# Down projections of a two-layer decoder trunk: 10 of 22 row blocks as 2x2 block products with seven multiplications, placed among the gate and up products of later chunks

## The chip, the cores and the metric

The kernel runs on 1 core of one Trainium2 chip. The metric is the device time of one execution in microseconds, as the median of several runs; one further execution was taken with the hardware profiler, and its trace is what this text reads.

## The reference

The trunk has two layers over 256 tokens of width 1024. Each layer is a feed-forward block (FFN), a mixer and a second FFN, each followed by a layer norm. The change is in the four FFNs, each of which is `swiglu` with 2816 hidden columns.

```python
def swiglu(x, w_gu, w_down):
    g, u = jnp.split(x @ w_gu, 2, axis=-1)
    return (jax.nn.silu(g) * u) @ w_down

def reference(x, ln_g, ln_b, ffn_w_gu, ffn_w_down, ...):
    for l in range(DEPTH):                       # 2
        x = layer_norm(ALPHA * x + 0.5 * swiglu(x, ffn_w_gu[l, 0], ffn_w_down[l, 0]), ln_g[l, 0], ln_b[l, 0])
        ...                                      # y: attention and gating (layer 0), mLSTM (layer 1)
        x = layer_norm(ALPHA * x + y, ln_g[l, 1], ln_b[l, 1])
        x = layer_norm(ALPHA * x + 0.5 * swiglu(x, ffn_w_gu[l, 1], ffn_w_down[l, 1]), ln_g[l, 2], ln_b[l, 2])
    return x
```

## The kernel before

All activations stay on the chip: `xTh` and `xTl` hold the transposed activation (1024 x 256), `xn` the natural one (2 halves `t` of 128 tokens x 1024). Every large product is made of three matmuls (`mm3`): each fp32 operand is split in a high part rounded to fp32r and a low part that is the rest, and high x high, high x low and low x high are summed in PSUM. The weights' split is work on the chip too: `split` lets ACT cast the high part (`whi`) and DVE subtract it (`wlo`).

**Weights** come as a stream `W` of blocks of 128 x 1024 (512 KB), numbered `n` in the order in which TensorE (PE) uses them. `w_dma(n)` loads a block into one of `RAW` = 6 buffers on SP's queue, `w_split(n)` splits it into one of `RING` = 9 slots (`whi`, `wlo`), and `w_done(n)`, called when the last matmul of a block has been written down, splits block n + 9 and loads block n + 15. So a slot that PE frees is refilled at once with the block that PE wants nine blocks later.

**An FFN** (`ffn`) has 22 chunks of 128 hidden columns. The first 2 or 4 are made as groups (`post`), while the previous layer norm ends. `chunk(c)` makes one of the others: 24 matmuls of 256 columns for gate into a PSUM bank of tag `m` (3 banks), a silu on ACT, 24 for up, the product of the two on DVE (tile `hp`), and its split into the `hT` of that chunk. Then `out_proj` is the down projection: for each of the 22 row blocks c and each half t of the tokens, `hT[c, t]` is the stationary operand and 512 columns of the weight block the moving one, 12 matmuls of 512 columns for a block, into four PSUM banks of tag `a` (`acc[t][h]`). The last 7 blocks (`skew`) are taken bank by bank, so that the layer norm of one half starts while PE still works on the other.

**The other parts** are `layer_norm` (DVE, with its transposes on PE into tag `a`), `mixer_ab` and `mixer_c`; side work is written as generators that `tick` advances between products. The instructions of PE, DVE, ACT and GpSimd are put in their final order by the framework's scheduler from priorities in the order of the code; the order on SP is that of the code. `page` gives one of `PAGES` = 26 buffers of 516 columns.

Of the kernel before, what the change touches and what calls it, by code (L numbers as in the profile page):

```python
# [14 lines left out]
P = 128  # L15
# [5 lines left out]
FC = 22  # L21
ALPHA = 4.0 ** 0.25
EPS = 1e-5
RING = 9
RAW = 6
PAGES = 26
NWARM = 7


@with_exitstack  # L30
def trunk(ctx, tc, W, F_d, x_d, g_d, b_d, rope_d, id_d, idb_d, mk_d, tri_d, sel_d,
# [125 lines left out]
    def feed(i):  # L157
        if i < KC:
            st[i] = wpool.tile([P, 1024], F32, tag="raw", name="raw", bufs=RAW)
            if i == 0:  # L160
                nc.sync.dma_start(out=st[i][:, 0:256], in_=F_d[i][:, 0:256])
                nc.scalar.dma_start(out=st[i][:, 256:768], in_=F_d[i][:, 256:768])
            else:
                nc.sync.dma_start(out=st[i][:, 0:768], in_=F_d[i])
        else:
            w_dma(i - KC + 4)

    for i in range(RAW):
        feed(i)
# [1 line left out]
    for i in range(KC):  # L171
        j, o = divmod(i, 2)
        if o == 0:
            whi[j] = wpool.tile([P, 1024], F32R, tag="hi", name="whi", bufs=RING)
            wlo[j] = wpool.tile([P, 1024], F32R, tag="lo", name="wlo", bufs=RING)
# [33 lines left out]
    def layer_norm(t, acc, scale, eps, k, last=False, segs=((0, 512), (512, 512))):  # L209
        st = small("lnst", [P, 3, 6])  # L210
        mv = small("lnmv", [P, 2])
        for i, (o, w) in enumerate(segs):
            if i < 2:
                sl = xn[:, t, i * 512:(i + 1) * 512]
                nc.vector.scalar_tensor_tensor(out=sl, in0=sl, scalar=scale, in1=acc[i], op0=OP.mult, op1=OP.add)  # L215
# [97 lines left out]
        return spawn(layer_norm(1, acc[1], scale, eps, k, last))  # L313

    def ffn(n0, k, ln_prev, last=False):
        hT = {}
        head = 1 if ln_prev is None else 2

        def post(g, t, ps):
            hp = pages.tile([P, 2, 256], F32, tag="h", name="hp", bufs=3)  # L320
# [9 lines left out]
            split(pt, q[:, 0], q[:, 1])  # L330

        def chunk(c):
            n = n0 + 4 * head + 2 * (c - 2 * head)
# [6 lines left out]
            nc.vector.tensor_tensor(out=hp[:, 1, :], in0=hp[:, 0, :], in1=pu, op=OP.mult)  # L340
            q = page("hT", [P, 2, S], F32R)
            split(hp[:, 1, :], q[:, 0], q[:, 1])
            for t in range(2):
                w = slice(t * P, (t + 1) * P)
                hT[c, t] = (q[:, 0, w], q[:, 1, w])
# [37 lines left out]
    def mixer_ab(n0, k, ln_prev):
        sgb = cpool.tile([P, 2, 512], F32, name="sgb")
# [4 lines left out]
        bcast(sgb[:, 0, :], sg_d, 0, 512)  # L389
        bcast(sgb[:, 1, :], sb_d, 0, 512)  # L390
# [95 lines left out]
        def sgu_v(ps, t):  # L486
# [71 lines left out]
    def mixer_c(n0, k, ln_prev):  # L558
        va, qkT, gate, num, cat, cc = {}, {}, {}, {}, {}, {}
        pTs, hst, done = {}, {}, set()  # L560
        hgp = cpool.tile([P, 2, 512], F32, name="sgb")
        hg = [hgp[:, i, :] for i in range(2)]
# [13 lines left out]
        def gates(ps):  # L576
# [16 lines left out]
            yield 2  # L593
# [172 lines left out]
def _arrays(np, i):  # L766
# [4 lines left out]

    def ffn(l, f, head):
        w = i["ffn_w_gu"][l, f]
        gu = w.reshape(4, 2, P, 2, FG, 256).transpose(4, 0, 2, 1, 3, 5)
        parts.append(gu[0:head].reshape(4 * head, P, 1024))
        gc = w.reshape(8, P, 2, FC, P).transpose(3, 2, 1, 0, 4)
        parts.append(gc[2 * head:].reshape(2 * (FC - 2 * head), P, 1024))
        parts.append(i["ffn_w_down"][l, f].reshape(FC, P, 1024))
# [83 lines left out]
```

## Time and profile before

| | |
|---|---|
| median of 3 runs | 969.52 us (969.33 to 969.57) |
| the profiled execution | 969.82 us, span of the instructions 968.1 us |
| PE busy | 956.7 us, 99% of the span |
| weight loads of PE (PEld) | 857.3 us, 89% |
| DVE busy | 599.1 us, 62% |
| ACT busy | 455.8 us, 47% |
| from HBM | 180.97 MB, 188 GB/s over the span |

The span is what the trace shows, from the first instruction of the program to the last; the execution's own time is 1.7 us longer. PE is called busy while a matmul is in flight, and one matmul's time in flight is longer than the step from its start to the next one's start, so a matmul's cost is read from starts.

### The profile page before, as it was taken

To read this page: it belongs to the slowest core of one execution; us is meant where nothing else is said; L and a number is where in the kernel's file an instruction comes from. 1 tells how busy PE (TensorE), PEld (TensorE's weight loads), DVE (VectorE), ACT (ScalarE), POOL (GpSimd) and SP (SyncE) were. 2 spreads that over 40 slices of the span, in tenths; PEclk is the share of its full clock that TensorE was granted. 3 is DMA by queue.
4 is the path that set the end of the run, shared out by engine and by line. 5 is a ranking of instruction groups with operands and counts; after the bars stand their busy time and mean duration, and the time that the engine had idled before them with its cause. 6 is when DMAs were issued, how large, how long until landed. Compare 5 with 4: busy or idle time off the path is not lost.

```text
span 968.1 us, 15564 instructions
## 1 busy us (share of the span) xinstructions
PE 956.7 (99%) x6226; PEld 857.3 (89%) x6226; DVE 599.1 (62%) x829; ACT 455.8 (47%) x657; POOL 22.3 (2%) x28
## 2 busy tenths in 40 slices
PE   9999999999999999999999999999999999999997
PEld 7999988887888999988889999888888789999885
DVE  7575554685777555544875555438767876555435
ACT  6564443345645444443354444325675445445320
POOL 0000000000100000000000000001000000000000
PEclk9999999999999999999999999999999999999999
DMA  9885666484446656666466565656644467666611
GB/s 349 307 299 182 192 188 187 159 275 150 140 135 219 225 190 183 194 186 188 169 238 181 191 191 182 194 152 219 217 131 126 137 216 230 187 194 182 189 45 44
DMA packets 52072, 183.03 MB, mean 189 GB/s; under 512 B 6176, under 2 KB 6688, under 8 KB 51872
## 3 DMA queue, kind: packets, MB, share of 16 engines
q1 hardware_dynamic: 51856, 181.77, 58.2%
q8 instruction: 49, 0.80, 0.3%
q10 hardware_dynamic: 144, 0.26, 0.1%
q14 instruction: 23, 0.19, 0.1%
HBM read 180.97 MB, written 1.05 MB: 188 GB/s over the span
## 4 chain that ended last, share of the span: by engine, by line
PE 70%; DVE 2%; POOL 0%; issue 0%; ACT 0%; DVEq 0%
PE ps_m L120 15%; PE ps_m L121 15%; PE ps_m L122 15%; PE ps_a L121 8%; PE ps_a L120 8%; PE ps_a L122 8%; DVE wlo L93 1%; PE ps_a L237 1%; POOL hrs L206 0%; PE ps_t L326 0%; ACT whi L92 0%; PE ps_a L503 0%; DVE hst L684 0%; DVE num L711 0%; PE ps_a L665 0%
## 5 line engine op out<-in xcount | busy, mean ns | idle before, releaser
L93 DVE TENSOR_TENSOR wlo<-raw,whi 128x1024 fp32r<-128x1024 f32 (+1 forms) x327 | 393.9, 1212 | 231.8 <-ACT whi L92 230.4
L92 ACT CAST whi<-raw 128x1024 fp32r<-128x1024 f32 (+1 forms) x327 | 339.9, 1043 | 378.4 <-PE ps_m L121 190.6
L120 PE MATMUL ps_m<-xTh,whi 128*128 128x256 f32 x1280 | 358.6, 280 | 1.4 <-DVE qkc L651 1.4
L121 PE MATMUL ps_m<-xTl,whi 128*128 128x256 f32 x1280 | 357.8, 280 | 0.0
L122 PE MATMUL ps_m<-xTh,wlo 128*128 128x256 f32 x1280 | 357.4, 279 | 0.0
L120 PEld LDWEIGHTS ps_m<-xTh,whi 128*128 128x128 f32 x1280 | 240.6, 188 | 2.1 <-ACT cch L92 1.6
L121 PEld LDWEIGHTS ps_m<-xTl,whi 128*128 128x128 f32 x1280 | 240.6, 188 | 0.6 <-issue 0.3
L122 PEld LDWEIGHTS ps_m<-xTh,wlo 128*128 128x128 f32 x1280 | 240.6, 188 | 0.2 <-issue 0.2
L120 PE MATMUL ps_a<-whi,hT 128*128 128x512 f32 (+1 forms) x352 | 138.2, 392 | 0.0
L121 PE MATMUL ps_a<-wlo,hT 128*128 128x512 f32 (+1 forms) x352 | 138.0, 392 | 0.0
L122 PE MATMUL ps_a<-whi,hT 128*128 128x512 f32 (+1 forms) x352 | 137.9, 392 | 0.0
L120 PE MATMUL ps_m<-whi,xTh 128*128 128x512 f32 x224 | 90.7, 405 | 0.0
L121 PE MATMUL ps_m<-wlo,xTh 128*128 128x512 f32 x224 | 89.3, 399 | 0.0
L122 PE MATMUL ps_m<-whi,xTl 128*128 128x512 f32 x224 | 88.6, 396 | 0.0
L122 PEld LDWEIGHTS ps_a<-whi,hT 128*128 128x128 f32 x352 | 66.1, 188 | 15.2
L120 PEld LDWEIGHTS ps_a<-whi,hT 128*128 128x128 f32 x352 | 66.1, 188 | 15.1
L121 PEld LDWEIGHTS ps_a<-wlo,hT 128*128 128x128 f32 x352 | 66.1, 188 | 15.0
L340 DVE TENSOR_TENSOR hp<-hp,ps_m 128x256 f32<-128x256 f32 x74 | 31.2, 421 | 51.0 <-PE ps_m L122 50.9
L122 PEld LDWEIGHTS ps_m<-whi,xTl 128*128 128x128 f32 x224 | 42.1, 188 | 9.6
L120 PEld LDWEIGHTS ps_m<-whi,xTh 128*128 128x128 f32 x224 | 42.2, 188 | 9.1
L121 PEld LDWEIGHTS ps_m<-wlo,xTh 128*128 128x128 f32 x224 | 42.2, 188 | 8.7
L215 DVE SCALAR_TENSOR_TENSOR xn<-xn,ps_a 128x512 f32<-128x512 f32 x24 | 16.0, 682 | 37.5 <-PE ps_a L122 37.4
(197 smaller groups left out, 601.3 us busy)
## 6 DMA issues: line engine op xcount, KB each, us to landing
raw<-in_W SPq DMA_DIRECT2D x320, 512.0 KB, 4.2
gb<-in_g SPq DMA_DIRECT2D x6, 512.0 KB, 3.9
gb<-in_b SPq DMA_DIRECT2D x6, 512.0 KB, 4.8
raw<-in_F SPq DMA_DIRECT2D x7, 384.0 KB, 5.5
xn<-in_x SPq DMA_DIRECT2D x1, 1024.0 KB
out<-xn SPq DMA_DIRECT2D x4, 256.0 KB, 2.0
swt<-in_sw SPq DMA_DIRECT2D x2, 256.0 KB, 7.7
sgb<-in_hg SPq DMA_DIRECT2D x2, 256.0 KB, 5.3
```

The costliest lines, as they stand in the source:

```text
L92: nc.scalar.copy(out=hi, in_=src)
L93: nc.vector.tensor_tensor(out=lo, in0=src, in1=hi.bitcast(F32), op=OP.subtract)
L120: mm_(out=out, lhsT=lh, rhs=rh, start=start, stop=False)
L121: mm_(out=out, lhsT=lh, rhs=rl, start=False, stop=False)
L122: mm_(out=out, lhsT=ll, rhs=rh, start=False, stop=stop)
L215: nc.vector.scalar_tensor_tensor(out=sl, in0=sl, scalar=scale, in1=acc[i], op0=OP.mult, op1=OP.add)
L237: nc.tensor.transpose(pt[:, c, :], sl[:, c * P:(c + 1) * P], ident)
L340: nc.vector.tensor_tensor(out=hp[:, 1, :], in0=hp[:, 0, :], in1=pu, op=OP.mult)
```

## The change

Blocks 4 to 13 of the 22 row blocks of each down projection leave `out_proj` and are taken in 5 pairs. Two row blocks (even chunk e, odd chunk o) times two halves of the tokens are a 2x2 block matrix of `hT`; two row blocks times two quarters of 256 output columns are a 2x2 block matrix of the weights. Their product, four 128 x 256 blocks, is made from seven block products in place of eight (the variant with 15 additions). Since the output has four quarters, a pair is taken twice, for `r` = 0 (columns 0 to 511) and `r` = 1 (512 to 1023): 20 pairs, 40 calls of `pair` in the kernel.

The additions on the hidden side are made in `chunk` (tile `hs`, four 128 x 128 operations after the odd chunk), those on the weights' side in `refill` (tile `tt`), and those on the results in `fold`, which adds the four banks of a round into `xn`. `ffn_plan` puts `pair(0, p)` behind chunk 7 + 2p and `pair(1, p)` behind chunk 16 + p. A paired weight block holds the four 128 x 256 quarters of both row blocks, and its split takes two slots: 768 columns of plain quarters and 1024 of sums. `RING` goes from 9 to 8, `RAW` from 6 to 5, `PAGES` from 26 to 30; `w_done` refills as many blocks as there are free slots. In `mixer_c` the generators `norm(t, 0)` are started behind the third chunk of the second group instead of behind the fourth of the first, and one `yield` is longer; the mixers' tiles `sgb` move into pages.

```diff
-RING = 9
-RAW = 6
-PAGES = 26
+RING = 8
+RAW = 5
+PAGES = 30
+NP = 5
+C0 = 4
...
+PAIRS = range(C0, C0 + 2 * NP, 2)
+PLAIN = [c for c in range(FC) if not C0 <= c < C0 + 2 * NP]
+SLOTS = {}
+for _p in range(NP):
+    SLOTS.setdefault(C0 + 2 * _p + 3, []).append((0, _p))
+    SLOTS.setdefault(C0 + 2 * NP + 2 + _p, []).append((1, _p))
...
+    def refill():
+        while ring["split"] < NG and ring["free"] >= (2 if paired(ring["split"]) else 1):
...
+            if paired(n):
+                yh, yl = slot()
+                tt = wpool.tile([P, 4, 256], F32, tag="tt", name="tt", bufs=TT)
+                bb = r.rearrange("p (a n) -> p a n", a=4)
+                sub = nc.vector.tensor_tensor
+                sub(out=tt[:, 0:2, :], in0=bb[:, 0:1, :].to_broadcast([P, 2, 256]), in1=bb[:, 1:3, :], op=OP.subtract)
+                split(r[:, 256:1024], hi[:, 0:768], lo[:, 0:768])
+                sub(out=tt[:, 2, :], in0=bb[:, 2, :], in1=tt[:, 0, :], op=OP.subtract)
+                sub(out=tt[:, 3, :], in0=bb[:, 3, :], in1=tt[:, 2, :], op=OP.subtract)
+                split(tt.rearrange("p a n -> p (a n)"), yh, yl)
...
     def w_done(n):
+        ring["free"] += 2 if paired(n) else 1
         del whi[n], wlo[n]
-        w_split(n + RING)
-        w_dma(n + RING + RAW)
+        refill()
...
+                tt(out=hs[:, 4, :], in0=hs[:, 0, :], in1=hs[:, 2, :], op=OP.add)
+                tt(out=hs[:, 5, :], in0=hs[:, 4, :], in1=hs[:, 1, :], op=OP.subtract)
+                tt(out=hs[:, 6, :], in0=hs[:, 0, :], in1=hs[:, 1, :], op=OP.subtract)
+                tt(out=hs[:, 7, :], in0=hs[:, 3, :], in1=hs[:, 5, :], op=OP.subtract)
+                for lo, hi in ((1, 5), (5, 8)):
...
+                    split(hs[:, lo:hi, :], qh, ql)
...
+        def pair(r, p):
+            n = at["pair", r, p]
+            if p == 0:
+                acc[r] = [bank_a((P, 2, 256)) for _ in range(4)]
+            a = acc[r]
+            for i, half, col, b, h in ((1, 0, 0, 2, 0), (3, 0, 2, 0, 0), (7, 0, 1, 0, 1), (2, 1, 3, 1, 0),
+                                       (4, 1, 0, 1, 1), (5, 1, 2, 2, 1), (6, 1, 1, 3, 0)):
+                w = slice(256 * col, 256 * col + 256)
+                rh, rl = whi[n][half][:, w], wlo[n][half][:, w]
+                lh, ll = hS[p, i]
+                o = a[b][:, h, :]
+                mm_(out=o, lhsT=lh, rhs=rh, start=p == 0 and h == 0, stop=False, skip_group_check=True)
+                mm_(out=o, lhsT=lh, rhs=rl, start=False, stop=False, skip_group_check=True)
+                mm_(out=o, lhsT=ll, rhs=rh, start=False, stop=p == NP - 1, skip_group_check=True)
+            w_done(n)
+            tick()
+            if p == NP - 1:
+                fold(r, a)
...
+            nc.scalar.copy(out=x[:, 0, :], in_=a[2][:, 0, :])
+            tt(out=u[:, 0, :], in0=x[:, 0, :], in1=a[2][:, 1, :], op=OP.add)
+            tt(out=u[:, 1, :], in0=u[:, 0, :], in1=a[3][:, 0, :], op=OP.add)
+            tt(out=x[:, 1, :], in0=u[:, 0, :], in1=a[1][:, 1, :], op=OP.add)
+            stt = nc.vector.scalar_tensor_tensor
+            stt(out=x0, in0=x0, scalar=2.0 * ALPHA, in1=a[1], op0=OP.mult, op1=OP.add)
+            stt(out=x1, in0=x1, scalar=2.0 * ALPHA, in1=a[0], op0=OP.mult, op1=OP.add)
+            tt(out=x0, in0=x0, in1=u[:, 1:2, :].to_broadcast([P, 2, 256]), op=OP.add)
+            tt(out=x1, in0=x1, in1=x, op=OP.add)
...
-        return out_proj(FC, n0 + 4 * FG, lhs, 7, k, 2.0 * ALPHA, 4.0 * EPS, last)
+        return out_proj(len(PLAIN), at["down", PLAIN[0]], lhs, 7, k, None, 4.0 * EPS, last)
...
-            for t in range(2):
-                norms[t, g] = spawn(norm(t, g))
...
+                if g == 1 and i == 2:
+                    for t in range(2):
+                        norms[t, 0] = spawn(norm(t, 0))
+            if g == 1:
+                for t in range(2):
+                    norms[t, 1] = spawn(norm(t, 1))
```

How the instructions stand is shown at three places. The first is PE in the second FFN, at the end of chunk 15 (bank `ps_m_4026` before, `ps_m_4435` now, its up product). Before, the gate product of chunk 16 follows at once:

```order
L122 MATMUL ps_m_4026<-xTh_72,wlo_3748 128x256
L120 MATMUL ps_m_4062<-xTh_72,whi_3779 128x256
L121 MATMUL ps_m_4062<-xTl_73,whi_3779 128x256
L122 MATMUL ps_m_4062<-xTh_72,wlo_3780 128x256
L120 MATMUL ps_m_4062<-xTh_72,whi_3779 128x256
```

Now the 21 matmuls of `pair(0, 4)` stand between the two; the first ten and the last one are:

```order
L171 MATMUL ps_m_4435<-xTh_72,wlo_4213 128x256
L429 MATMUL ps_a_3763<-whi_4272,hSh_4291 128x256
L430 MATMUL ps_a_3763<-wlo_4273,hSh_4291 128x256
L431 MATMUL ps_a_3763<-whi_4272,hSl_4292 128x256
L429 MATMUL ps_a_3761<-whi_4272,hSh_4291 128x256
L430 MATMUL ps_a_3761<-wlo_4273,hSh_4291 128x256
L431 MATMUL ps_a_3761<-whi_4272,hSl_4292 128x256
L429 MATMUL ps_a_3761<-whi_4272,hSh_4295 128x256
...
L431 MATMUL ps_a_3764<-whi_4274,hSl_4296 128x256
L169 MATMUL ps_m_4516<-xTh_72,whi_4320 128x256
```

The bank changes every third matmul, the stationary operand is a piece of `hS`, and 256 columns of a weight block move.

The second place is DVE in the same stretch. Before, the product of chunk 15 (`hp_3993`) is followed by one weight split for each product of PE:

```order
L340 TENSOR_TENSOR hp_3993<-hp_3993,ps_m_4026 128x256
L93 TENSOR_TENSOR wlo_4052<-raw_3851,whi_4051 128x1024
L93 TENSOR_TENSOR hT_4058<-hp_3993,hT_4058 128x256
L93 TENSOR_TENSOR wlo_4088<-raw_3887,whi_4087 128x1024
L340 TENSOR_TENSOR hp_4061<-hp_4061,ps_m_4094 128x256
```

Now the split of a paired block (`wlo_4492`, then `wlo_4494` from `tt_4495`) and the fold of round 0 (lines 445 to 452) stand there:

```order
L392 TENSOR_TENSOR hp_4402<-hp_4402,ps_m_4435 128x256
L142 TENSOR_TENSOR wlo_4461<-raw_4284,whi_4460 128x1024
L142 TENSOR_TENSOR hT_4467<-hp_4402,hT_4467 128x256
L142 TENSOR_TENSOR wlo_4492<-raw_4324,whi_4491 128x768
L445 TENSOR_TENSOR fu_4506<-fx_4505,ps_a_3763 128x256
L142 TENSOR_TENSOR wlo_4494<-tt_4495,whi_4493 128x1024
L446 TENSOR_TENSOR fu_4506<-fu_4506,ps_a_3764 128x256
L447 TENSOR_TENSOR fx_4505<-fu_4506,ps_a_3762 128x256
L449 SCALAR_TENSOR_TENSOR xn_74<-xn_74,ps_a_3762 128x512
L450 SCALAR_TENSOR_TENSOR xn_74<-xn_74,ps_a_3761 128x512
L451 TENSOR_TENSOR xn_74<-xn_74,fu_4506 128x512
L452 TENSOR_TENSOR xn_74<-xn_74,fx_4505 128x512
```

The scheduler has put the second half of the split between the first two operations of the fold, so the banks come free behind it.

The third place is DVE in `mixer_c`, at the conv operations (`qkc`) on the first chunk of the second group. Before:

```order
L93 TENSOR_TENSOR wlo_7358<-raw_7119,whi_7357 128x1024
L93 TENSOR_TENSOR ccl_7369<-ps_t_7363,cch_7368 128x512
L711 TENSOR_TENSOR num_7220<-num_7220,gate_6904 128x2x256
L651 SCALAR_TENSOR_TENSOR qkc_7404<-ps_m_7322,cw_83,qkc_7404 128x255
L651 SCALAR_TENSOR_TENSOR qkc_7404<-ps_m_7322,cw_83,qkc_7404 128x254
L93 TENSOR_TENSOR wlo_7422<-raw_7169,whi_7421 128x1024
L651 SCALAR_TENSOR_TENSOR qkc_7404<-ps_m_7322,cw_83,qkc_7404 128x253
```

And now:

```order
L142 TENSOR_TENSOR wlo_8032<-raw_7854,whi_8031 128x1024
L760 SCALAR_TENSOR_TENSOR qkc_8050<-ps_m_7996,cw_83,qkc_8050 128x255
L820 TENSOR_TENSOR num_7919<-num_7919,gate_7597 128x2x256
L760 SCALAR_TENSOR_TENSOR qkc_8050<-ps_m_7996,cw_83,qkc_8050 128x254
L142 TENSOR_TENSOR wlo_8068<-raw_7947,whi_8067 128x1024
L760 SCALAR_TENSOR_TENSOR qkc_8050<-ps_m_7996,cw_83,qkc_8050 128x253
```

The split `ccl` of the first transposed norm result has left this place for a later one; the rest of the norm's work has stayed.

## Rows read from the trace of the kernel before

**Rows 1.** Page: busy time (us), share, instructions; PE and granted clock by slice.
```profile
PE 956.7 (99%) x6226; PEld 857.3 (89%) x6226; DVE 599.1 (62%) x829; ACT 455.8 (47%) x657; POOL 22.3 (2%) x28
...
PE   9999999999999999999999999999999999999997
...
PEclk9999999999999999999999999999999999999999
```

**Rows 2.** Stages, us: gate/up, down, norm with `mixer_ab`, `mixer_c`. Columns head the fence.
```profile
core 0: us, PE busy (x) PEld busy (x) DVE busy (x) ACT busy (x) POOL busy (x), PEclk, DMA share, GB/s
...
320.00:410.00 90.00, 90.00 (x774) 90.00 (x773) 51.68 (x65) 43.30 (x65) 0.00 (x0) 1.00 0.60 188
...
425.00:470.00 45.00, 45.00 (x195) 36.40 (x194) 20.21 (x22) 14.73 (x15) 0.92 (x1) 1.00 0.51 153
...
180.00:220.00 40.00, 40.00 (x188) 32.54 (x187) 36.60 (x53) 19.75 (x23) 3.19 (x4) 1.00 0.73 240
...
690.00:770.00 80.00, 77.87 (x455) 66.65 (x455) 57.08 (x127) 44.21 (x74) 5.53 (x5) 1.00 0.41 129
```

**Rows 3.** PE timeline, gate/up: first and last of 174 matmuls (start us, us).
```profile
319.80 0.28 PE L122 MATMUL ps_m<-xTh,wlo 128*128 128x256 f32 x1
...
339.98 0.28 PE L121 MATMUL ps_m<-xTl,whi 128*128 128x256 f32 x1
```

**Rows 4.** PE timeline, down projection: first and last of 195 matmuls.
```profile
424.74 0.40 PE L121 MATMUL ps_a<-wlo,hT 128*128 128x512 f32 x1
...
469.77 0.39 PE L120 MATMUL ps_a<-whi,hT 128*128 128x512 f32 x1
```

**Rows 5.** PE timeline, end of last down projection: first and last of 42.
```profile
955.84 0.28 PE L120 MATMUL ps_a<-whi,hT 128*128 128x256 f32 x1
...
960.69 0.28 PE L122 MATMUL ps_m<-whi,hT 128*128 128x256 f32 x1
```

**Rows 6.** Groups by line, engine, shape: busy us, mean ns of one, idle before.
```profile
L93 DVE TENSOR_TENSOR wlo<-raw,whi 128x1024 fp32r<-128x1024 f32 x320 | 389.1, 1223 | 231.5 <-ACT whi L92 230.4
L340 DVE TENSOR_TENSOR hp<-hp,ps_m 128x256 f32<-128x256 f32 x74 | 31.2, 421 | 51.0 <-PE ps_m L122 50.9
...
L215 DVE SCALAR_TENSOR_TENSOR xn<-xn,ps_a 128x512 f32<-128x512 f32 x24 | 16.0, 682 | 37.5 <-PE ps_a L122 37.4
...
L410 DVE TENSOR_TENSOR ra<-ra,rb 128x512 f32<-128x512 f32 x4 | 2.7, 686 | 0.0
...
L514 DVE TENSOR_TENSOR mix<-mix,uT 128x128 f32<-128x128 f32 x8 | 2.1, 283 | 0.0
...
L92 ACT CAST whi<-raw 128x1024 fp32r<-128x1024 f32 x320 | 335.6, 1052 | 378.4 <-PE ps_m L121 190.6 <-PE ps_a L122 150.5 <-PE ps_m L122 22.5
L92 ACT CAST hT<-hp 128x256 fp32r<-128x256 f32 x74 | 29.5, 399 | 8.7 <-DVE hp L340 8.7
```

**Rows 7.** DVE timeline: one gate/up chunk; two splits without a wait between.
```profile
347.13 0.42 DVE L340 TENSOR_TENSOR hp<-hp,ps_m 128x256 f32<-128x256 f32 x1 [0.68 <-PE ps_m L122]
...
350.83 1.23 DVE L93 TENSOR_TENSOR wlo<-raw,whi 128x1024 fp32r<-128x1024 f32 x1 [1.24 <-ACT whi L92]
352.73 0.42 DVE L340 TENSOR_TENSOR hp<-hp,ps_m 128x256 f32<-128x256 f32 x1 [0.68 <-PE ps_m L122]
...
26.81 2.35 DVE L93 TENSOR_TENSOR wlo<-raw,whi 128x1024 fp32r<-128x1024 f32 x2
```

**Rows 8.** `mixer_c`, DVE and PE timelines: PE's longest wait after the start.
```profile
727.89 0.68 DVE L93 TENSOR_TENSOR ccl<-ps_t,cch 128x512 fp32r<-128x512 f32 x1
...
731.75 0.35 PE L120 MATMUL ps_m<-xTh,whi 128*128 128x256 f32 x1 [1.42 <-DVE qkc L651]
```

**Rows 9.** Start, DVE and PE timelines: first two whole blocks, first use.
```profile
14.69 2.49 DVE L93 TENSOR_TENSOR wlo<-raw,whi 128x1024 fp32r<-128x1024 f32 x2 [0.90 <-ACT whi L92]
...
16.67 0.28 PE L120 MATMUL ps_m<-xTh,whi 128*128 128x256 f32 x1
```

**Rows 10.** Page: the weight load of a 256-column matmul in gate/up.
```profile
L121 PEld LDWEIGHTS ps_m<-xTl,whi 128*128 128x128 f32 x1280 | 240.6, 188 | 0.6 <-issue 0.3
```

More of the change, by code (lines that the diff above doesn't have):

```diff
@@ L23, with ffn_plan @@
 EPS = 1e-5
-RING = 9
-RAW = 6
-PAGES = 26
-NWARM = 7
+RING = 8
[3 more added lines that the diff above has]
+C0 = 4
+NWARM = 7
+TT = 2
+PAIRS = range(C0, C0 + 2 * NP, 2)
[4 more added lines that the diff above has]
+    SLOTS.setdefault(C0 + 2 * NP + 2 + _p, []).append((1, _p))
+def ffn_plan(head):
+    plan = [("group", g, j) for g in range(head) for j in range(4)]
+    for c in range(2 * head, FC):
+        plan += [("gate", c), ("up", c)]
+        plan += [("pair", r, p) for r, p in SLOTS.get(c, [])]
+    return plan + [("down", c) for c in PLAIN]
 @with_exitstack
@@ L71, in trunk, with paired, w_dma @@
     raw, whi, wlo = {}, {}, {}
-    def w_dma(n):
+    stream = {}
+    for n0, head in ((0, 1), (94, 2), (160, 2), (258, 2)):
+        for i, e in enumerate(ffn_plan(head)):
+            if e[0] == "pair":
+                stream[n0 + i] = e
+    ring = {"free": RING, "split": 4, "dma": 4}
+    def paired(n):
+        return n in stream
+    def w_dma():
+        n = ring["dma"]
         if n < NG:
@@ L173, in trunk @@
         if o == 0:
[L174 to L175 removed]
+            whi[j], wlo[j] = slot()
         w = slice(o * 512, (o + 1) * 512)
@@ L188, in trunk @@
             nc.sync.dma_start(out=ident, in_=id_d)
-    for n in range(4, RING):
-        w_split(n)
-        w_dma(n + RAW)
+    refill()
     nc.sync.dma_start(out=xn, in_=x_d)
@@ L339, in chunk @@
             proj_t(n + 1, pu)
[L340 to L345 removed]
+            if c in PLAIN:
+                nc.vector.tensor_tensor(out=hp[:, 1, :], in0=hp[:, 0, :], in1=pu, op=OP.mult)
+                q = page("hT", [P, 2, S], F32R)
+                split(hp[:, 1, :], q[:, 0], q[:, 1])
+                for t in range(2):
+                    w = slice(t * P, (t + 1) * P)
+                    hT[c, t] = (q[:, 0, w], q[:, 1, w])
+                return
@@ new lines, in chunk @@
+            o = (c - C0) % 2
+            if o == 0:
+                cur["hs"] = wpool.tile([P, 8, P], F32, tag="hs", name="hs", bufs=1)
+            hs = cur["hs"]
+            nc.vector.tensor_tensor(out=hs[:, 2 * o:2 * o + 2, :].rearrange("p a n -> p (a n)"), in0=hp[:, 0, :], in1=pu,
+                                    op=OP.mult)
+            if o == 1:
+                tt = nc.vector.tensor_tensor
+                tt(out=hs[:, 4, :], in0=hs[:, 0, :], in1=hs[:, 2, :], op=OP.add)
[3 more added lines that the diff above has]
+                for lo, hi in ((1, 5), (5, 8)):
+                    qh = page("hSh", [P, hi - lo, P], F32R)
+                    ql = page("hSl", [P, hi - lo, P], F32R)
+                    split(hs[:, lo:hi, :], qh, ql)
+                    for i in range(lo, hi):
+                        hS[(c - C0) // 2, i] = (qh[:, i - lo, :], ql[:, i - lo, :])
@@ new lines, in fold @@
+        def fold(r, a):
+            x = page("fx", [P, 2, 256])
+            u = page("fu", [P, 2, 256])
+            tt = nc.vector.tensor_tensor
+            w = slice(512 * r, 512 * r + 512)
+            x0 = xn[:, 0, w].rearrange("p (a n) -> p a n", a=2)
+            x1 = xn[:, 1, w].rearrange("p (a n) -> p a n", a=2)
+            nc.scalar.copy(out=x[:, 0, :], in_=a[2][:, 0, :])
[7 more added lines that the diff above has]
+            tt(out=x1, in0=x1, in1=x, op=OP.add)
@@ L373, in ffn @@
             chunk(c)
+            for r, p in SLOTS.get(c, []):
+                pair(r, p)
         def lhs(c, t):
+            c = PLAIN[c]
             if (c, t) not in hT:
@@ L560, in mixer_c @@
         pTs, hst, done = {}, {}, set()
-        hgp = cpool.tile([P, 2, 512], F32, name="sgb")
-        hg = [hgp[:, i, :] for i in range(2)]
+        hg = [page("hg", [P, 512]) for i in range(2)]
         wif = page("wif", [P, 64])
@@ L773, in ffn @@
         w = i["ffn_w_gu"][l, f]
[L774 to L778, printed above, removed]
+        gu = w.reshape(4, 2, P, 2, FG, 256).transpose(4, 0, 2, 1, 3, 5).reshape(FG, 4, P, 1024)
+        gc = w.reshape(8, P, 2, FC, P).transpose(3, 2, 1, 0, 4).reshape(FC, 2, P, 1024)
+        wd = i["ffn_w_down"][l, f].reshape(FC, P, 4, 256)
+        for e in ffn_plan(head):
+            if e[0] == "group":
+                v = gu[e[1], e[2]]
+            elif e[0] in ("gate", "up"):
+                v = gc[e[1], int(e[0] == "up")]
+            elif e[0] == "down":
+                v = wd[e[1]].reshape(P, 1024)
+            else:
+                o, q = 2 * e[1], C0 + 2 * e[2]
+                v = np.concatenate([wd[q][:, o + 1], wd[q][:, o], wd[q + 1][:, o + 1], wd[q + 1][:, o]], axis=1)
+            parts.append(v[None])
     def cols(w):
```

48 lines of the change are left out of this document (30 added, 18 removed).

## The prediction

> **What bounds the kernel now.** I read the page's busy times first, then the busy time by stage, then the starts of single matmuls. PE is busy for 956.7 of 968.1 us and its clock is granted in full in every slice [rows 1]: the kernel is one long stream of matmuls. By stage it is the same: in gate/up and in the down projection PE has no gap at all, while DVE works 51.68 of 90 us and 20.21 of 45 us; only around the norms and in the mixers is DVE nearly full (36.60 of 40 us), and in `mixer_c` PE loses 2.1 of 80 us [rows 2]. So a matmul that is left out of an FFN gives its step back, as long as nothing else comes late there.
>
> The step from one matmul's start to the next one's is the price. In gate/up 174 matmuls of 256 columns start in 20.18 us, which is 173 steps of 116.6 ns [rows 3]. In the down projection 195 of 512 columns start in 45.03 us, 194 steps of 232.1 ns [rows 4]. At the end of the last down projection 42 matmuls take 256 columns of the weights with `hT` stationary: 41 steps in 4.85 us, 118.3 ns [rows 5]. A matmul of half the columns costs half, and nearly nothing for being one more.
>
> **PE's part.** Two row blocks cost 2 x 12 matmuls of 512 columns: 24 x 232.1 ns = 5.57 us. A pair costs two rounds of 21 matmuls of 256 columns. Their operands are those of the last stretch [rows 5] (a piece of `hT` stationary, 256 columns of a weight block moving), so I take 118.3 ns: 42 x 118.3 = 4.97 us. That is 0.60 us less for each of 20 pairs: **-12.0 us**. By gate/up's 116.6 ns it would be 4.90 us and -13.5 us; this is the good end. That the bank changes every third matmul is nothing new, since the down projection does so too.
>
> The Trainium skill speaks against this: "TensorE: Matmul & The Clock Gate", section "Back-to-back issue gap", says that in a real stream of weight loads and matmuls both set the spacing, and gives about 81 ns for 128 columns and 131 ns for 512. On a straight line between these, 256 columns would take an estimated 98 ns, a pair 4.1 us against 3.1 us for its two blocks, and the kernel would be about 19 us slower, near 989. The rows don't bear this out: 116.6 and 118.3 ns stand against 232.1 ns, a ratio of one half.
>
> **DVE's and ACT's part.** Prices are group means [rows 6]: 1.22 us for 1024 columns, 0.69 for 512, 0.42 for 256, 0.28 for 128; for 768 I take the middle of 512 and 1024, 0.95. A paired block costs DVE 0.69 + 2 x 0.42 (sums) + 0.95 + 1.22 (splits) = 3.70 us instead of 1.22. The hidden side of a pair costs 4 x 0.28 + 0.69 + 0.55 = 2.4 us instead of 2 x 0.42. A fold costs 3 x 0.42 + 2 x 0.68 + 2 x 0.69 = 4.0 us. Together at most 40 x 2.48 + 20 x 1.5 + 8 x 4.0 = 161 us more: DVE goes from 599 to some 740 to 760 us of 955. (Work that waits for nothing follows closer: two splits take 2.35 us instead of 2.45 [rows 7].) ACT gets 40 casts of 768 columns, by a line between 0.40 and 1.05 us some 0.83 us each, and about 10 us of smaller work: 456 to 500 us. Both hide behind PE, if they also do so locally:
> - Round 0 repeats two chunks and a `pair`: PE 96 x 116.6 + 21 x 118.3 ns = 13.7 us; DVE 4 x 1.22 + 2 x 0.42 + 3.70 + 2.4 = 11.8 us, 86%.
> - Round 1 repeats one chunk and a `pair`: PE 8.1 us; DVE 2 x 1.22 + 2 x 0.42 + 3.70 = 7.0 us, 86%.
>
> DVE stays below PE in both, so a delay doesn't grow. A block is still refilled far ahead: behind a `pair`, the eight slots hold four plain blocks, the next pair and two more, so what is split then is used 13.7 us later; even if it is done 6 us after its slot came free, 7 us are left. Loads: 5 blocks in 13.7 us are 191 GB/s and 3 in 8.1 us are 195, against 188 now and 240 in the norm's stretch, where PE doesn't wait [rows 2].
>
> **The folds** are the tight place. Round 1, and after it `out_proj`, need the four `a` banks that a fold has to read, and PE asks for them one chunk after the last `pair` of a round: 48 x 116.6 ns = 5.6 us. Count from that pair's last matmul, in DVE's order as it stands in the diff's second place: the hidden product, one split and `hT` of chunk 15 end by 0.2. The 768-column split, whose slot came free with the pair's first products and whose cast ends near -0.1, ends at 1.2; the first sum at 1.6; the 1024-column split, whose cast ends at 1.4, at 2.8; two sums at 3.6; the two operations that free the last banks at 4.3 and 5.0. With the overlap of back-to-back work [rows 7] it is 4.5. At the fold of round 1 a 1024-column split stands in place of the 768-column one: 4.8 to 5.3. Bank by bank, PE needs the last of them a little after 5.6. So the folds cost **0**, with only 0.3 to 1.4 us to spare; I keep up to 3 us for all eight.
>
> **`mixer_c`.** PE's longest wait after the start is 1.42 us, for the third conv operation behind DVE's norm work [rows 8]. The 0.68 us split `ccl` no longer stands ahead of it, so I take **-0.6 us**. It could be -1.4 (all of the wait), or +1.5, since the same work now falls on the stretch ahead of the output projection, and a ring of eight slots lets DVE work less far ahead.
>
> **Start.** With five raw buffers a load waits for the split of five blocks before it, not six. The first two whole blocks are split at 14.69 to 17.18 us, the first of them by about 15.9, and PE begins at 16.67 [rows 9]: 0.8 us to spare, about what one step of the splits takes. I take **+0.2 us**, and up to 1.
>
> **Sum.** 969.8 - 12.0 - 0.6 + 0.2 = 957.4 us for a profiled execution; the median lies 0.3 below it: **957.1 us**. The best ends together give 969.5 - 13.5 - 1.4 = 954.6, the worst 969.5 - 12.0 + 1.5 + 1 + 3 = 963.0.
>
> **Rivals.**
> - *PE waits at the folds.* If DVE reaches each fold about 2 us later than I worked out, PE waits some 1 us eight times: 965. For it: DVE's order is fixed, with the splits between the fold's steps, and at 86% it has little room. Against it: three chunks stand between a fold and any other hard date of DVE, and DVE waits 0.7 and 1.2 us in each chunk now [rows 7], so it enters with nothing left over. Chance 0.20.
> - *Slower: the folds eat it all.* The same place decides it: the gain of 12.4 us is gone when each of eight folds holds PE for 1.55 us, which is DVE 2.5 us late, two more 1024-column splits ahead of each fold. At three more (3.7 us late) PE loses 8 x 2.8 = 22 us, and the time is 979. It would need sums that cost DVE half as much again as the group means say. Chance 0.06.
> - *A fixed part for each matmul.* The pair breaks even at 5.57 us / 42 = 132.6 ns a matmul. If the weight load, 188 ns [rows 10], set the pace, 42 x 188 = 7.90 us, 2.33 us more for each pair: 1016. Against it: gate/up has the same load for each 256 columns and steps at 116.6 ns, two loads at a time. Chance 0.02.
> - *No change.* That the scheduler puts the new matmuls elsewhere is excluded by the order, where each pair's 21 stand together. A smaller gain could meet losses of equal size: 0.05.
> - *Better than the good end*, below 954: waits in the mixers that I don't see. 0.05.
>
> **Numbers.** My forecast, 954 to 960.5, has 0.62. The range from 953.8 to 964 takes in the bounds of the unknown costs and the milder half of the first rival. A difference of 0.2%, 1.9 us, is about what a measurement of this kernel can tell from none. Faster: 0.62 + 0.20 + 0.05 = 0.87; within it 0.05; slower 0.06 + 0.02 = 0.08.
>
> **What would show it.** In the changed kernel's trace, 840 matmuls of 256 columns into `ps_a` from `hSh` and `hSl`, at 118 ns from start to start (117 at best), and 480 fewer of 512. PE's busy time near 945 us and still 99% of the span. DVE at 740 to 760 us, ACT near 500. No idle time of PE ahead of the first matmuls of round 1 (`ps_a` waiting for `xn`, `fx` or `fu`) and of the down projection; the last bank freed 4.5 to 5.3 us after a round's last pair. In `mixer_c`, PE's wait for `qkc` at 0.8 us or less. I am wrong if a pair's matmuls step at more than 120 ns, if PE waits for DVE at the folds, or if weights (`wlo`) come to be what PE waits for.

## The result, and the profile after

The changed kernel takes **959.22 us** (958.57 to 960.43, 4 runs) against 969.55 us, a ratio of 0.9895 (95% interval 0.9882 to 0.9907). That is 10.3 us less, where 12.4 were forecast. Its profiled execution took 959.6 us, with a span of 957.9 us.

The page's busy times, which answer to [rows 1]:

```profile
PE 946.4 (99%) x6586; PEld 867.2 (91%) x6586; DVE 732.5 (76%) x1125; ACT 495.6 (52%) x705; POOL 21.0 (2%) x28
...
PEclk9999999999999999999999999999999999999999
```

TensorE lost 10.3 us of busy time and is still the bound. VectorE took on 133 us and ScalarE 40 us of work, of which nearly nothing shows in the span. The windows of round 0 and round 1 in the second FFN, and of `mixer_c` (columns as in [rows 2]):

```profile
core 0: us, PE busy (x) PEld busy (x) DVE busy (x) ACT busy (x) POOL busy (x), PEclk, DMA share, GB/s
333.20:388.20 55.00, 55.00 (x471) 55.00 (x470) 45.30 (x71) 30.54 (x41) 0.00 (x0) 1.00 0.61 190
388.20:428.70 40.50, 40.50 (x346) 40.50 (x346) 33.55 (x46) 23.17 (x31) 0.00 (x0) 1.00 0.61 199
...
690.00:760.00 70.00, 68.48 (x387) 57.51 (x386) 51.75 (x118) 37.89 (x65) 3.70 (x5) 1.00 0.36 116
```

PE has no gap in either round, with VectorE busy for 82 and 83% of the time (86% was worked out). The PE timeline at the end of round 0 shows the first and last of a pair's 21 matmuls, the first of chunk 16 behind it, and the first of round 1:

```profile
388.25 0.28 PE L429 MATMUL ps_a<-whi,hSh 128*128 128x256 f32 x1
...
390.63 0.28 PE L431 MATMUL ps_a<-whi,hSl 128*128 128x256 f32 x1
390.75 0.28 PE L169 MATMUL ps_m<-xTh,whi 128*128 128x256 f32 x1
...
396.35 0.29 PE L429 MATMUL ps_a<-whi,hSh 128*128 128x256 f32 x1
```

From the first start of the pair to that of the chunk are 21 steps in 2.50 us, 119.0 ns each; the chunk's 48 take 5.60 us, 116.7 ns each. Over all 840 matmuls of pairs the mean is 118.70 ns. The fold that follows, on VectorE's timeline:

```profile
390.94 0.95 DVE L142 TENSOR_TENSOR wlo<-raw,whi 128x768 fp32r<-128x768 f32 x1
391.81 0.41 DVE L445 TENSOR_TENSOR fu<-fx,ps_a 128x256 f32<-128x256 f32 x1
392.14 1.22 DVE L142 TENSOR_TENSOR wlo<-tt,whi 128x1024 fp32r<-128x1024 f32 x1
393.27 0.41 DVE L446 TENSOR_TENSOR fu<-fu,ps_a 128x256 f32<-128x256 f32 x1
393.60 0.41 DVE L447 TENSOR_TENSOR fx<-fu,ps_a 128x256 f32<-128x256 f32 x1
393.94 0.68 DVE L449 SCALAR_TENSOR_TENSOR xn<-xn,ps_a 128x512 f32<-128x512 f32 x1
394.53 0.68 DVE L450 SCALAR_TENSOR_TENSOR xn<-xn,ps_a 128x512 f32<-128x512 f32 x1
```

The last bank is free at 395.21, which is 4.58 us after the pair's last matmul, and PE asks at 5.72 us: 1.1 us to spare. At the other seven folds the last bank comes free 4.58 to 4.88 us after the pair. Groups of VectorE that were not there before (mean ns of one in the middle, idle before at the end):

```profile
L142 DVE TENSOR_TENSOR wlo<-raw,whi 128x768 fp32r<-128x768 f32 x40 | 38.1, 952 | 11.3 <-ACT whi L141 11.3
L124 DVE TENSOR_TENSOR tt<-raw 128x512 f32<-128x512 f32 x40 | 27.5, 687 | 24.0 <-DMA raw<-in_W 24.0
...
L142 DVE TENSOR_TENSOR hSl<-hs,hSh 128x384 fp32r<-128x384 f32 x20 | 11.0, 551 | 0.0
```

The prices are those of the prediction (0.95, 0.69, 0.55 us). What the prediction left out is at the end of the second row: the first subtraction waits 24.0 us in all for a weight block that has not landed. Of PE's waits, the first row answers to [rows 8] and the second is new; behind them VectorE's timeline at the head of the third FFN, and PE's:

```profile
PE ps_m L169 <- DVE qkc L760: 0.9, 1, 0.9
PE ps_t L377 <- DVE hp L373: 0.5, 1, 0.5
```

```profile
497.82 0.69 DVE L124 TENSOR_TENSOR tt<-raw 128x512 f32<-128x512 f32 x1 [1.39 <-DMA raw<-in_W]
498.43 1.22 DVE L142 TENSOR_TENSOR wlo<-raw,whi 128x1024 fp32r<-128x1024 f32 x1
499.57 0.41 DVE L373 TENSOR_TENSOR hp<-hp,ps_m 128x256 f32<-128x256 f32 x1
```

```profile
500.04 0.44 PE L377 MATMUL ps_t<-ident,hp 128*128 128x128 f32 x2 [0.47 <-DVE hp L373]
```

VectorE stands still for 1.39 us because the block is late, and the hidden product that PE's transposes want is queued behind it: 0.47 us of PE.

### The profile page after: what moved, and what is told of

It reads as the page before. It is cut to its first block, busy times and chain, and to the rows that moved or that the text cites. A ratio compares the mean times of both kernels' runs of the same rounds, so it can differ in the third digit from the quotient of the medians.

```text
span 957.9 us, 16624 instructions
## 1 busy us (share of the span) xinstructions
PE 946.4 (99%) x6586; PEld 867.2 (91%) x6586; DVE 732.5 (76%) x1125; ACT 495.6 (52%) x705; POOL 21.0 (2%) x28
## 4 chain that ended last, share of the span: by engine, by line
PE 70%; DVE 2%; DMA 1%; issue 1%; ACT 1%; POOL 0%; DVEq 0%
PE ps_m L169 15%; PE ps_m L170 15%; PE ps_m L171 15%; PE ps_a L169 5%; PE ps_a L170 5%; PE ps_a L171 5%; PE ps_a L430 3%; PE ps_a L431 3%; PE ps_a L429 3%; DVE wlo L142 1%; PE ps_a L286 1%; DMA raw<-in_W 1%; ACT whi L141 0%; PE ps_t L377 0%; PE ps_a L613 0%
## 5 line engine op out<-in xcount | busy, mean ns | idle before, releaser
L141 ACT CAST whi<-raw 128x1024 fp32r<-128x1024 f32 (+2 forms) x327 | 331.0, 1016 | 258.9 <-PE ps_a L171 77.2
L142 DVE TENSOR_TENSOR wlo<-raw,whi 128x1024 fp32r<-128x1024 f32 (+2 forms) x327 | 380.9, 1176 | 89.2 <-ACT whi L141 86.4
L171 PEld LDWEIGHTS ps_m<-xTh,wlo 128*128 128x128 f32 x1280 | 240.5, 188 | 0.6 <-DVE wlo L142 0.4
L430 PE MATMUL ps_a<-wlo,hSh 128*128 128x256 f32 x280 | 78.8, 281 | 0.0
L429 PE MATMUL ps_a<-whi,hSh 128*128 128x256 f32 x280 | 78.8, 281 | 0.0
L431 PE MATMUL ps_a<-whi,hSl 128*128 128x256 f32 x280 | 78.8, 281 | 0.0
L169 PE MATMUL ps_a<-whi,hT 128*128 128x512 f32 (+1 forms) x192 | 75.3, 392 | 0.0
L170 PE MATMUL ps_a<-wlo,hT 128*128 128x512 f32 (+1 forms) x192 | 75.0, 390 | 0.0
L171 PE MATMUL ps_a<-whi,hT 128*128 128x512 f32 (+1 forms) x192 | 74.9, 390 | 0.0
L430 PEld LDWEIGHTS ps_a<-wlo,hSh 128*128 128x128 f32 x280 | 52.8, 189 | 0.0
L431 PEld LDWEIGHTS ps_a<-whi,hSl 128*128 128x128 f32 x280 | 52.8, 188 | 0.0
L429 PEld LDWEIGHTS ps_a<-whi,hSh 128*128 128x128 f32 x280 | 52.7, 188 | 0.0
```

Source lines behind the costliest of these rows:

```text
L142: nc.vector.tensor_tensor(out=lo, in0=src, in1=hi.bitcast(F32), op=OP.subtract)
L169: mm_(out=out, lhsT=lh, rhs=rh, start=start, stop=False)
L170: mm_(out=out, lhsT=lh, rhs=rl, start=False, stop=False)
L171: mm_(out=out, lhsT=ll, rhs=rh, start=False, stop=stop)
L429: mm_(out=o, lhsT=lh, rhs=rh, start=p == 0 and h == 0, stop=False, skip_group_check=True)
L430: mm_(out=o, lhsT=lh, rhs=rl, start=False, stop=False, skip_group_check=True)
```

## The experiments

My theory was that the gain is the matmuls left out and nothing else, that all added work is hidden, and that the 2 us missing from the forecast lie in slightly longer steps and in that wait. The rivals: part of the gain or loss belongs to the smaller buffers, to the mixer's new order or to moving blocks under gate/up; the work added on VectorE and ScalarE slows PE's steps; the folds have no real slack.

**Eight products in place of seven.**

```diff
-            for i, half, col, b, h in ((1, 0, 0, 2, 0), (3, 0, 2, 0, 0), (7, 0, 1, 0, 1), (2, 1, 3, 1, 0),
-                                       (4, 1, 0, 1, 1), (5, 1, 2, 2, 1), (6, 1, 1, 3, 0)):
+            for i, half, col, b, h in ((0, 0, 1, 1, 0), (0, 0, 0, 1, 1), (2, 0, 3, 1, 0), (2, 0, 2, 1, 1),
+                                       (1, 0, 1, 0, 0), (1, 0, 0, 0, 1), (3, 0, 3, 0, 0), (3, 0, 2, 0, 1)):
```

> The changed kernel with all eight block products of a pair (24 matmuls of 256 columns in a round in place of 21), no sums on the hidden or the weights' side, two banks in place of four and a fold of two operations; the blocks stay where the change put them. My theory, that the gain is the products left out and nothing else: 120 matmuls more than the changed kernel, 120 x 118.7 ns = 14.2 us, 959.2 + 14.2 = 973.4 us, some 2 to 4 us above the kernel before (48 x 118.7 = 5.70 us a pair against 5.57, twenty times, is 2.6). If the changed kernel's sums also slow TensorE's steps, 1 to 2 us less, about 972. Rival (the gain comes from moving a part of the down projection under gate/up, where VectorE has more time): at or below 969.5 us.

With the eighth product all sums go, and two of the four banks of a round. Measured 972.73 us, ratio to before 1.0032 (1.0019 to 1.0044). The page:

```profile
PE 960.1 (99%) x6706; PEld 881.2 (91%) x6706; DVE 607.9 (63%) x825; ACT 454.0 (47%) x637; POOL 20.8 (2%) x28
```

So moving the blocks under gate/up gains nothing: this kernel takes 3.0 us more than the one before (2.6 expected). Of that, 2.5 us are the price of narrower matmuls, from starts: 960 of 256 columns take 113.9 us, and the 480 of 512 columns that went took 111.4. Leaving out one product in eight, 120 matmuls, is worth 13.5 us (14.2 expected), with all the sums that it needs. The products left out are the whole gain.

**No sums on the weights' side.** All seven products read plain quarters, so the down projections' values are others.

```diff
-                split(r[:, 256:1024], hi[:, 0:768], lo[:, 0:768])
...
-                split(tt.rearrange("p a n -> p (a n)"), yh, yl)
-                whi[n], wlo[n] = (hi, yh), (lo, yl)
+            split(r, hi, lo)
+            whi[n], wlo[n] = ((hi, hi), (lo, lo)) if paired(n) else (hi, lo)
```

> The changed kernel without the sums of weight blocks: all seven products use plain quarters of the block, so the down projections' values are not the reference's; TensorE has the same 6586 matmuls, VectorE loses the three subtractions and a quarter more of the split for 40 paired blocks (about 40 x 2.5 = 100 us), ScalarE some 33 us, and a paired block takes one slot. My theory (all of that is hidden): 959.2 less the 0.5 us wait at the head of the third feed-forward, 958.7 us, pair steps 118.7 ns. Rival (the work of VectorE and ScalarE slows TensorE's steps by memory contention, which is where the missing 2 us went): the 256-column steps of gate/up go back from 117.5 to 117.2 ns and the pairs' from 118.7 to 118.0, 957 us or less.

Measured 958.22 us (ratio 0.9881, 0.9867 to 0.9894), 1.0 us less than the changed kernel, with intervals that overlap. VectorE is busy for 654.3 us in place of 732.5, but PE's steps hardly move: 118.61 ns in the pairs, 117.45 in gate/up (118.70 and 117.52 in the changed kernel). The 0.5 us wait is not in this trace. The rival that VectorE's work slows PE falls: taking 78 us of it away gives back 0.3 us of steps. The rest of the 1.0 us is not in the FFNs' steps. In this trace the third matmul of the first chunk starts at 16.4 us; in the changed kernel's two traces it starts at 16.8 and 17.3.

**The smaller buffers alone**, in the kernel before.

```diff
-RING = 9
-RAW = 6
+RING = 8
+RAW = 5
```

> The kernel before with RING 8 in place of 9 and RAW 5 in place of 6, nothing else. My theory: the start costs 0.1 to 0.3 us and nothing else, 969.7 us. Rival (the shorter ring is where part of the products' gain went): 970.5 to 972 us, with TensorE waiting for wlo or for the mixer's work.

Measured 969.79 us, ratio 1.0000 (0.9991 to 1.0009): nothing. Gate/up's step is 117.27 ns, as before (117.24).

**The mixer's old order**, in the changed kernel.

```diff
-            yield 3
+            yield 2
...
-                if g == 1 and i == 2:
-                    for t in range(2):
-                        norms[t, 0] = spawn(norm(t, 0))
+            for t in range(2):
+                norms[t, g] = spawn(norm(t, g))
```

> The changed kernel with the mLSTM mixer's norm work put back where it stood before (started behind the fourth chunk of the first group, shorter yield). My theory: the move is worth 0.4 to 0.6 us, so this kernel takes 959.2 + 0.5 = 959.7 us and TensorE's wait for qkc goes from 0.9 back to about 1.4 us. Rival (the move brought nothing, or cost something in the stretch ahead of the output projection): 959.2 us or less, with the wait for qkc longer but another one shorter.

Measured 959.14 us (ratio 0.9889, 0.9876 to 0.9903). The wait for `qkc` is back at 1.4 us, as expected, but the time is the same. 0.5 us is below what these runs can tell, so the move's worth stays open; it is not the 1.4 us of the good end.

**A later fold**, three and nine operations more (`range(10)` in the second kernel).

```diff
-            tt(out=u[:, 0, :], in0=x[:, 0, :], in1=a[2][:, 1, :], op=OP.add)
+            for _ in range(4):
+                tt(out=u[:, 0, :], in0=x[:, 0, :], in1=a[2][:, 1, :], op=OP.add)
```

> The changed kernel with the first sum of each fold made four times in place of once (three more VectorE operations of 0.42 us at most, 1.1 to 1.3 us, ahead of the operations that free the banks; the result is the same). My theory: a fold has a slack of 0.85 to 1.2 us (last bank freed 4.6 to 4.9 us after the round's last pair, TensorE asks at 5.75), so TensorE begins to wait, 0 to 0.4 us a fold: 959.2 to 962 us. Rival (TensorE is held by something ahead of the banks, or VectorE's order has no slack at all): each fold costs the full 1.2 us, 959.2 + 8 x 1.2 = 968.8; or, if the banks are not what TensorE asks for, nothing at all, in the next kernel too.

> As the kernel with three more operations a fold, but nine more (3.4 to 3.8 us). My theory: the slack of about 1.0 us is used up and the rest stands in TensorE's way at all eight folds, 8 x (3.6 - 1.0) = 21 us: 980 us, between 976 and 984, and PE's waits name xn, fu or fx at the first matmuls of round 1 and of the down projection; this is the rival of the prediction in which the folds eat the gain. Other way: VectorE catches up elsewhere and the waits are shorter, 965 to 972 us; or longer than the delay, since the weights' splits stand behind the fold on VectorE, over 988 us.

Measured 959.22 us (ratio 0.9888, 0.9873 to 0.9904) and 958.87 us (0.9893, 0.9880 to 0.9907): nothing, twice, where my theory said 0 to 3 and 21 us. The timelines of the second kernel at the first fold, VectorE's and then PE's:

```profile
109.73 0.41 DVE L446 TENSOR_TENSOR fu<-fx,ps_a 128x256 f32<-128x256 f32 x1
...
118.68 0.42 DVE L446 TENSOR_TENSOR fu<-fx,ps_a 128x256 f32<-128x256 f32 x1
...
120.54 0.68 DVE L450 SCALAR_TENSOR_TENSOR xn<-xn,ps_a 128x512 f32<-128x512 f32 x1
```

```profile
114.33 0.28 PE L429 MATMUL ps_a<-whi,hSh 128*128 128x256 f32 x1
...
115.04 0.29 PE L169 MATMUL ps_m<-xTh,whi 128*128 128x256 f32 x1
...
119.49 0.28 PE L429 MATMUL ps_a<-whi,hSh 128*128 128x256 f32 x1
...
120.68 0.28 PE L429 MATMUL ps_a<-whi,hSh 128*128 128x256 f32 x1
...
121.74 0.28 PE L429 MATMUL ps_a<-whi,hSh 128*128 128x256 f32 x1
```

The fold does come later: the last bank is free at 121.2, 12.7 us after the pair. But the scheduler has written another order for PE. It takes 6 of the 21 matmuls at 114.33, for the bank that is free, then 38 of the next chunk, and the rest of the pair in pieces of 6, 6 and 3 (from 119.49, 120.68 and 121.74) as banks come free. A late fold that the scheduler knows of is covered by gate/up work, as long as there is some. So these two kernels did not measure the slack that I had worked out. The next one takes the cover away.

**No chunk between the second fold and the down projection.**

```diff
-    SLOTS.setdefault(C0 + 2 * NP + 2 + _p, []).append((1, _p))
+    SLOTS.setdefault(C0 + 2 * NP + 3 + _p, []).append((1, _p))
```

> The changed kernel with round 1 one chunk later, so that its last pair stands behind the last chunk and the down projection asks for the banks at once, with no chunk to cover the second fold. My theory (the chunk between is what hides a fold): TensorE waits in each of the four feed-forwards, at least until the first bank is free (the first sum ends some 1.9 us after the pair) and at most until the last one (4.9 us): 959.2 + 4 x 1.9 to 4 x 4.9 = 967 to 979 us, the lower end if the down matmuls can be ordered by banks as they come free. Rival (the order that the scheduler makes hides a late fold anyway, as with nine more operations): 959 to 961 us.

Measured 965.74 us (ratio 0.9962, 0.9950 to 0.9975), 6.5 us more than the changed kernel. First a row of PE's waits, then PE's timeline at the first of the four places, and VectorE's, with the operation that PE waits for:

```profile
PE ps_a L169 <- DVE fu L445: 4.9, 3, 1.7
```

```profile
154.69 0.28 PE L431 MATMUL ps_a<-whi,hSl 128*128 128x256 f32 x1
156.60 0.50 PE L169 MATMUL ps_a<-whi,hT 128*128 128x512 f32 x1 [1.63 <-DVE fu L445]
```

```profile
156.13 0.42 DVE L445 TENSOR_TENSOR fu<-fx,ps_a 128x256 f32<-128x256 f32 x1
```

PE waits until the first sum has freed the first bank, and no longer: 1.91 us from start to start in place of 0.12, in three FFNs; in the last the step is 1.12 us, ahead of a `wlo`. Together 6.4 us, a little under the lower end of what I expected (7.6): the down matmuls are ordered by banks too.

**Three pairs, and six.**

```diff
-NP = 5
+NP = 3
```

```diff
-NP = 5
-PAGES = 30
-TT = 2
+NP = 6
+PAGES = 32
+TT = 1
...
+for _p, (_c0, _c1) in enumerate(((7, 17), (9, 18), (11, 19), (13, 19), (15, 20), (16, 20))):
```

> The changed kernel with NP = 3: three pairs in each feed-forward, 12 in all, in place of 20. My theory (a pair is worth 24 x 232.4 - 42 x 118.7 ns = 0.59 us, nothing fixed beside it): 8 x 0.59 = 4.7 us more than the changed kernel, 963.9 us. Rival (the gain of 10.3 us is 12 us less a fixed loss of some 2 us for having pairs at all, four stretches with a fold each twice): 969.5 - 12 x 0.60 + 2 = 964.3; rival (part of the gain comes from the shorter down projection as such or from the ring): 961 to 962.

> Six pairs in each feed-forward: round 0 behind chunks 7, 9, 11, 13, 15, 16, round 1 behind 17, 18, 19, 19, 20, 20, with one tt buffer in place of two and 32 pages in place of 30. My theory: 4 x 0.59 = 2.4 us less than the changed kernel if VectorE keeps up, 956.8 us. Against it: with two pairs behind a chunk TensorE has 48 x 116.6 + 42 x 118.7 ns = 10.6 us and VectorE 2.4 + 0.8 + 7.4 = 10.6 us, with nothing left over. Rival (weights come late): TensorE waits for wlo or for the fold in each of four feed-forwards by 0.6 us or more, 959.2 us or above.

Measured 963.13 us (0.9931, 0.9918 to 0.9943) and **955.80 us** (0.9857, 0.9844 to 0.9871), the fastest of all. With 0, 12, 20 and 24 pairs (the first is the kernel with the smaller buffers) the times are 969.8, 963.1, 959.2 and 955.8 us: 0.53 to 0.58 us a pair on average, and no fixed part that these times can tell. They don't tell more: from 12 to 20 pairs it is 0.5 us a pair and from 20 to 24 it is 0.9, and for three pairs a fixed loss would have made only 0.4 us, while the measured time lies 0.8 us below my forecast without one. Two windows of the six-pair kernel, round 1 up to the place where two pairs stand behind a chunk, and that place:

```profile
387.70:420.10 32.40, 32.40 (x279) 32.40 (x278) 29.35 (x45) 18.79 (x26) 0.00 (x0) 1.00 0.57 173
420.10:435.60 15.50, 15.50 (x135) 15.50 (x134) 13.38 (x19) 9.67 (x13) 0.00 (x0) 1.00 0.62 203
```

VectorE is 91% busy in the first and 86% in the second, not the 100% that I had worked out for the second: its load falls partly on the stretch ahead. PE has no gap.

**Six raw buffers, and the changed kernel once more.**

```diff
-RAW = 5
-TT = 2
+RAW = 6
+TT = 1
```

> The changed kernel with six raw buffers in place of five and one tt buffer in place of two. My theory: the wait of 0.5 us (1.1 us in the kernel with three more operations a fold) at the head of the third feed-forward is VectorE's wait for a late load, ahead of the hidden product that TensorE wants, and differs from execution to execution; with one more load under way it is gone, the times lie closer together, and the median is 0.2 to 0.8 us lower, 958.4 to 959.0. Rival (the wait comes from the tt buffers or from VectorE's order): no change, or slower with one tt buffer, 959.2 to 960.

> Six pairs in each feed-forward as in the kernel that took 955.8 us, with six raw buffers (31 pages in place of 32). If the loads are what is left to mend there (ScalarE waits 16.4 us and VectorE 6.0 us for raw in that trace, none of it passed on to TensorE at more than 0.3 us a time): 955.4 us, with less spread; if those waits are hidden already, 955.8 us.

> The changed kernel itself once more, beside the others on the same chip. 959.2 us; if the wait at the head of the third feed-forward differs from execution to execution, its profiled execution shows another length of it than 0.5 us, or none.

Measured 959.15 us (0.9891, 0.9876 to 0.9906) with six raw buffers, 956.59 (0.9864, 0.9851 to 0.9878) with six pairs as well, and 959.28 (0.9892, 0.9878 to 0.9905) for the changed kernel itself. With the sixth buffer, and one `tt` buffer fewer, nearly all of VectorE's wait for `raw` goes:

```profile
DVE tt L124 <- DMA raw<-in_W: 1.5, 3, 0.8
```

1.5 us in place of 24.0 (16.5 in the changed kernel's second trace), and the time does not change. The changed kernel's second trace has no wait at the head of the third FFN at all, and that of the three-operation kernel had 1.1 us there:

```profile
PE ps_t L377 <- DVE hp L373: 1.1, 1, 1.1
```

That execution took 961.87 us, the kernel's three others 958.82 to 959.38. So this wait is one of single executions, and the start is another: the first chunk began at 18.5 us there, and at 16.3 and 17.1 us in the changed kernel's two traces. With six pairs the sixth buffer gains nothing either; PE waits 1.1 us for ScalarE's first `whi` at the start of that profiled execution.

## Why the prediction came out, point by point

**Right: the bound and the mechanism.** A matmul of half the columns costs half, also from `hS` and with the bank changing every third time. The kernel with eight products shows that the gain is the product left out, and the kernels with 12, 20 and 24 pairs that it grows with the number of pairs.

**Mis-sized: PE's term.** -12.0 us came out as about -10.3. Three parts of it, from starts in the two traces. The pairs take 99.7 us where 840 x 118.3 = 99.4 were worked out. The 512-column steps of the down projections sum to 129.4 us in place of 240.5, 111.1 less, where 111.4 were worked out. And, with no term in the prediction, gate/up's 256-column steps rose from 117.24 to 117.52 ns over 3884 matmuls (waits left out), 1.1 us. Every kernel with pairs has this (117.38 to 117.53 ns; the two without have 117.24 and 117.27), also the one with eight products and no sums, so it is not VectorE's work. Nor is it spread evenly. PE's timeline shows the first matmul of gate/up behind each of the first two pairs of the first FFN, and the first of the pair that ends that stretch:

```profile
53.28 0.28 PE L169 MATMUL ps_m<-xTh,whi 128*128 128x256 f32 x1
...
64.59 0.28 PE L429 MATMUL ps_a<-whi,hSh 128*128 128x256 f32 x1
...
67.07 0.28 PE L169 MATMUL ps_m<-xTh,whi 128*128 128x256 f32 x1
...
78.27 0.28 PE L429 MATMUL ps_a<-whi,hSh 128*128 128x256 f32 x1
```

Each stretch is 96 steps: of 117.8 ns in the first, and in the second of 116.7, about as in [rows 3]. Of the 40 stretches behind a pair 14 step at 117.8 to 117.9 ns and 26 at 116.6 to 117.0; the 14 hold 912 matmuls, which at 1.1 ns more are 1.0 us, nearly all of the rise. The second trace has the same 14. All ten stretches of the third FFN step at 116.6 to 116.7, so putting two kinds of matmuls in turn is not enough to cause it. The level goes with the pair ahead: for each of the 20 pairs the stretch behind its round 0 and the one behind its round 1 are on the same level, though the weights, and mostly the length, differ (with eight products that holds for 19 of the 20). A stretch keeps its level to its end: with three pairs, the 336 matmuls behind the first FFN's last pair still step at 117.8 ns. What the two rounds of a pair share is their stationary operands, in the same buffers of `hS`. Whether the place of these sets the level no run tests; the cause stays open.

**Right: VectorE and ScalarE are hidden.** 732.5 and 495.6 us stand against 740 to 760 and 500. The prices were right; the sum was a little high, since starts follow closer.

**Right in the number, wrong in the reason: the folds.** They cost 0 and the last bank came free 4.58 to 4.88 us after the pair, against 4.5 to 5.3 worked out. But I called 0.3 to 1.4 us the whole room and let the first two rivals decide there. With nine operations more VectorE held banks to 12.7 us after the pair without any loss, since PE's order in that program is another one, with work of the next chunk ahead of the products that need those banks. That mechanism, at the prices given for it, was not there. What the folds need is other work for PE behind them: without it each second fold costs about 1.6 us (6.5 us over four).

**`mixer_c` and the start.** The wait for `qkc` went from 1.42 to 0.9 us, -0.5 for -0.6 (the bound of 0.8 given for the trace was missed by 0.1). At the start PE began its first chunk 0.4 us earlier (16.26 us for 16.67) and then lost 0.34 us to a wait for `wlo`, so it was level with before: 0 for +0.2. In the second trace it was 0.4 us behind. Neither term can be told in the medians.

**Not foreseen:** the 0.47 us wait at the head of the third FFN, which the second trace doesn't have. In the first trace it cancels what `mixer_c` gained.

**The two rivals by price.** A pair breaks even at 132.6 ns a matmul and runs at 118.7. The Trainium skill, "TensorE: Matmul & The Clock Gate", section "Back-to-back issue gap", from which the kernel was estimated at 989 us, does not hold for these matmuls: 512 columns step at a mean of 233.1 ns in the changed kernel's down projection, and 256 columns at half of that. The Trainium skill, "Perfetto Trace Analysis", section "Optimization Strategy", says that interleaving may help where the most-contended engine changes over time. Here it does not change: PE binds in gate/up and in the down projection, and the eight-product kernel, which moves the blocks and saves no product, gained nothing by it.

## What to carry to other kernels

Where one engine is busy for 99% of the span, work it in its own currency: count the instructions that a rewrite saves it, price them by start-to-start steps of a stretch with the same operands, and check only that the helpers stay under it locally. Here the moved work gained nothing by the move alone; undo the saving and keep the move, as with eight products here, to see which of the two pays. Here a late transfer of banks cost nothing as long as other work for the bound engine could stand behind it, and the order of that engine in the built program tells whether it does. One trace is not enough for terms of half a microsecond: waits of that size came and went between executions of the same program.

## What the runs showed of the hardware

The same gate/up products step at 116.7 or at 117.8 ns, a whole stretch at a time, at a granted clock of 1.00 on both levels; which of the two it is goes with the pair that ran ahead, and not with VectorE's load: 14 of 40 stretches are slow with VectorE busy for 732.5 us, and 13 of 40 with eight products, where it is 607.9 us. The pairs themselves step at 118.7 ns on average, and at 117.2 to 121.1 from pair to pair. And a sixth buffer, with which VectorE's wait for loads was 1.5 us in place of 24.0, moved the time by 0.1 us.
